# Five accumulating DMAs begun in the last part of the output projection instead of seven in the attention stage

## The chip, the cores and the metric

The kernel runs on one core of one Trainium2 chip. The metric is the device time of one execution in microseconds, given as a median over runs. Engines are named as in the profile: PE (TensorE matmul), PEld (TensorE weight load), DVE (VectorE), ACT (ScalarE), POOL (GpSimd) and SP (SyncE, which here only starts transfers).

## What is computed

One decoder layer on x of 256 tokens by 2048 channels, float32, batch 1:

```
h    = rmsnorm(x, pre_mix_g);  proj = h @ w_in             # 2048 x 4368
o_a  = sliding-window attention with sinks and ALiBi (16 heads)
o_b  = forgetting attention (16 heads, gate from proj)
mix  = concat(rmsnorm(o_a, grp_swa_g), rmsnorm(o_b, grp_fox_g)) @ w_out   # 2048 x 2048
x    = x + rmsnorm(mix, post_mix_g)
u    = causal_dwconv(rmsnorm(x, pre_ffn_g) @ w_up)          # 2048 x 11264, width 3
gate, val = split(u)
x    = x + rmsnorm((gelu(gate) * val) @ w_down, post_ffn_g)    # 5632 x 2048
```

## The kernel before

**Stages.** Weights stream from HBM in pieces of 512 KB through five buffers called `raw`; ACT rounds each to a high part `whi` and DVE makes the rest `wlo`, and PE multiplies with both. The order of the stages is w_in with both attentions (up to about 276 us), w_out (its first half of rows, for group A, from about 238 us, and its second half from about 276 to 334 us), w_up with convolution and GELU in two halves, each followed by two column passes over w_down.

**The sums of w_down blocks.** The column passes use a scheme with fewer products for 14 pairs of 128-row blocks of w_down, 7 in each half (`FAST`). For each pair it needs four combinations of quarter blocks, which are built in DRAM ahead of time: SP copies two blocks into scratch tensors `t13` and `t24` (line 87), and then POOL starts four accumulating DMAs (line 94) which add DRAM to DRAM: two from w_down into `t13`, one from `t13` into `t24`, and one within `t24`. The trace calls all of these `t`; in the order of the program the first pair has `t_74` (its t13) and `t_75` (its t24), the second pair `t_76` and `t_77`, and so on to `t_101`. The third add of a pair reads what the first wrote, and the fourth reads what the third wrote; POOL waits for these by the semaphores of the earlier adds before it starts the later one.

**What sets the place of an add.** `w_load` counts the weight loads. While the count lies in a span of `ADDS`, each load adds the span's pace to a debt, and when the debt reaches the size of the next add in the list (2 for 512 KB, 1 for 256 KB), that add is put into POOL's program there and kept in program order:

```
    def begin_some(steps, span):
        begin, end, pace = span
        if begin <= loads[0] < end:
            owed[span] = owed.get(span, 0) + pace
            while steps and owed[span] >= steps[0][0]:
                size, step = steps.pop(0)
                owed[span] -= size
                tc.keep_in_program_order(step())
```

The list is one for the whole kernel, so what one span doesn't take, the next one begins with. Loads 1 to 73 are of w_in, 74 to 89 of the first half of w_out's rows, 90 to 105 of the second half (four for each block of 512 output columns), and from 106 on of w_up.

**The second half of w_out.** `out_half(1, evac_b, range(2))` does column blocks 0 and 1. `evac_b` reads a finished bank: DVE adds it to the first half's result `mix` (line 792), ACT sums its squares (line 793), POOL multiplies it by the gain `gbc` (line 794). Blocks 2 and 3 are done in an order written out by hand for ACT, DVE and POOL: the piece (tokens 0, block 2), the piece (tokens 0, block 3), then `mix_rstd(0)`, whose last step is a power on POOL (line 239, `rmix`), then `residual(0, n)` for four n on DVE (line 812, `x_sb`), then `turn(0, n)`, which transposes `x_sb` on PE (line 819). PE's order is the program's. The same is done for tokens 1, and then w_up begins (lines 998, 1002, 340, 346), whose convolution has a multiply on POOL for each of 88 channel blocks (line 963).

Of the kernel before, what the change touches and what calls it, by code (L numbers as in the profile page):

```python
# [25 lines left out]
FHALF = 22  # L26
HOLD = 3
COPIES = (13, 91, 11 / 8)
ADDS = (30, 75, 1 / 4), (112, 282, 9 / 16)
FAST = (0, 2, 3, 4, 5, 6, 7)  # L30
FULL = (6, 7)

# [2 lines left out]
def hybrid_layer(ctx: ExitStack, tc: tile.TileContext, x, pre_mix_g, w_in, b_forget, sinks,  # L35
# [66 lines left out]
# [9 lines that stand above are left out]
    def w_load(src, a, c, pin=False):  # L111
# [5 lines left out]
        if not paused[0]:  # L117
            begin_some(copies, COPIES)
            for span in ADDS:
                begin_some(adds, span)  # L120
# [1284 lines left out]
```

## Time and profile before

| | |
|---|---|
| median of 3 runs | 1055.83 us (1054.78 to 1055.93) |
| the profiled execution, its own time | 1054.8 us |
| its span | 1053.1 us |
| busy: PE, DVE, ACT, POOL | 1041.0, 844.3, 659.8, 272.5 us |
| accumulating DMAs (line 94) | 56, of them 46 of 512 KB and 10 of 256 KB |

Times in the trace count from the start of the span. A row of the timeline gives start, duration, engine, line, operation, output and input names with shapes, how many, and in brackets the idle time of that engine before it with what ended it. A row of windows gives the stretch, its length, the busy time of each engine with the number of instructions, the granted clock of PE, the mean busy share of the 16 DMA engines and GB/s. "DMA to landing" is the time from the start of the issuing instruction to the arrival of the data.

### The profile page before, as it was taken

The page shows a single profiled execution, that of the slowest core. Times are in us where ns is not written, and L with a number is a line of the kernel's source. Part 1 is how long each engine was busy: PE and PEld are TensorE (multiplying, and loading weights), DVE is VectorE, ACT ScalarE, POOL GpSimd, SP SyncE. Part 2 cuts the span into 40 slices and gives each one's busy share as a digit, 9 for nine tenths or more (in the row PEclk, how much of TensorE's full clock was granted, in tenths as well). Part 3 has the DMA queues.
Part 4 walks back from the last instruction along what each step waited for, and adds up shares of the span by engine and source line. Part 5 has one row for each costly group of instructions (what it writes and reads, how often), then busy time and mean ns, then how long its engine had stood idle before and what let it go on. Part 6 is the DMA issues. An engine that isn't in the chain of part 4 may idle for free.

```text
span 1053.1 us, 16574 instructions
## 1 busy us (share of the span) xinstructions
PE 1041.0 (99%) x5854; PEld 907.6 (86%) x5854; DVE 844.3 (80%) x1370; ACT 659.8 (63%) x1126; POOL 272.5 (26%) x312
## 2 busy tenths in 40 slices
PE   9999999999999999999999999999999999999996
PEld 7889988888889988888888888888888888888885
DVE  5988887787467887788868799867788878779997
ACT  6766666676655865566556675646656666568771
POOL 4254325442022224232223000013223323210004
PEclk9999999999999999999999999999999999999999
DMA  8978999988872899899999796889999999969893
GB/s 281 314 246 289 295 300 308 359 251 303 319 257 68 265 252 260 230 269 240 228 242 265 259 410 196 290 234 222 287 223 247 254 230 257 235 221 387 292 419 130
DMA packets 177470, 279.98 MB, mean 266 GB/s; under 512 B 9052, under 2 KB 133244, under 8 KB 176124
## 3 DMA queue, kind: packets, MB, share of 16 engines
q1 hardware_dynamic: 162432, 249.51, 69.3%
q0 software_dynamic: 13952, 26.74, 17.3%
q10 hardware_dynamic: 1004, 2.68, 0.6%
q8 instruction: 46, 0.75, 0.3%
q14 instruction: 36, 0.29, 0.1%
HBM read 274.55 MB, written 57.69 MB: 315 GB/s over the span
## 4 chain that ended last, share of the span: by engine, by line
PE 89%; DVE 4%; DMA 3%; ACT 1%; POOL 1%; issue 1%; SPq 0%; DVEq 0%; POOLq 0%; ACTq 0%
PE bank_acc L340 16%; PE bank_att L340 14%; PE bank_acc L365 12%; PE bank_att L1044 10%; PE bank_acc L346 8%; PE bank_att L346 7%; PE bank_acc L309 7%; PE bank_acc L1044 5%; PE bank_acc L314 4%; DMA spare<-t 1%; PE bank_att L531 1%; PE bank_att L566 1%; DVE wlo L171 1%; PE bank_acc L1002 1%; DMA spare<-in_w_down_dram 1%; DVE wlo L369 1%
## 5 line engine op out<-in xcount | busy, mean ns | idle before, releaser
L171 DVE TENSOR_TENSOR wlo<-raw,whi 128x1024 fp32r<-128x1024 f32 (+3 forms) x271 | 335.8, 1251 | 94.7 <-ACT whi L168 86.4
L168 ACT CAST whi<-raw 128x1024 fp32r<-128x1024 f32 (+3 forms) x270 | 273.6, 1029 | 102.1 <-issue 43.8
L963 POOL TENSOR_TENSOR room<-room,rowf 128x256 f32<-128x256 f32 x88 | 97.7, 1132 | 331.3 <-DVE room L962 329.5
L340 PE MATMUL bank_acc<-hT,whi 128*128 128x512 f32 x736 | 173.3, 390 | 0.0
L340 PEld LDWEIGHTS bank_acc<-hT,whi 128*128 128x128 f32 x736 | 136.4, 188 | 27.4
L340 PE MATMUL bank_att<-hT,whi 128*128 128x512 f32 x640 | 150.6, 390 | 0.0
L340 PEld LDWEIGHTS bank_att<-hT,whi 128*128 128x128 f32 x640 | 118.7, 188 | 23.9
L967 ACT ACTIVATE room<-room,cw 128x256 f32<-128x256 f32 x88 | 52.7, 601 | 68.9 <-POOL room L963 68.6
L346 PEld LDWEIGHTS bank_acc<-hT,wlo 128*128 128x128 f32 x736 | 89.3, 188 | 2.0
L346 PE MATMUL bank_acc<-hT,wlo 128*128 128x256 f32 x736 | 89.9, 279 | 0.0
L309 PE MATMUL bank_acc<-hT,whi 128*128 128x512 f32 x352 | 88.0, 395 | 0.0
L1044 PE MATMUL bank_att<-whi,G 128*128 128x512 f32 x258 | 87.8, 389 | 0.0
L365 PE MATMUL bank_acc<-whi,oT 128*128 128x512 f32 (+1 forms) x272 | 81.7, 379 | 0.0
L346 PEld LDWEIGHTS bank_att<-hT,wlo 128*128 128x128 f32 x640 | 77.6, 188 | 1.7
L369 DVE TENSOR_TENSOR wlo<-raw,whi 128x1024 fp32r<-128x1024 f32 (+1 forms) x66 | 71.6, 1105 | 9.3 <-ACT whi L368 8.4
L346 PE MATMUL bank_att<-hT,wlo 128*128 128x256 f32 x640 | 77.9, 279 | 0.0
L973 DVE SCALAR_TENSOR_TENSOR room<-room,cw 128x256 f32<-128x256 f32 x88 | 60.2, 686 | 21.7 <-ACT room L967 21.7
L368 ACT CAST whi<-raw 128x1024 fp32r<-128x1024 f32 (+1 forms) x66 | 61.8, 953 | 22.5 <-DMA raw<-in_w_down_dram 5.7
L309 PEld LDWEIGHTS bank_acc<-hT,whi 128*128 128x128 f32 x352 | 63.3, 188 | 11.6
L365 PEld LDWEIGHTS bank_acc<-whi,oT 128*128 128x128 f32 x272 | 50.2, 188 | 9.3
L1044 PEld LDWEIGHTS bank_att<-whi,G 128*128 128x128 f32 x258 | 48.4, 188 | 10.0
L365 PE MATMUL bank_acc<-wlo,oT 128*128 128x512 f32 (+1 forms) x136 | 51.2, 377 | 0.0
(269 smaller groups left out, 1760.9 us busy)
## 6 DMA issues: line engine op xcount, KB each, us to landing
raw<-in_w_up_dram SPq DMA_DIRECT2D x176, 512.0 KB, 5.6
raw<-in_w_in_dram SPq DMA_DIRECT2D x51, 512.0 KB, 7.2
raw<-in_w_down_dram SPq DMA_DIRECT2D x45, 512.0 KB, 7.2
raw<-in_w_out_dram SPq DMA_DIRECT2D x32, 512.0 KB, 6.1
t<-in_w_down_dram POOLq DMA_DIRECT2D x28, 512.0 KB, 8.7
raw<-t SPq DMA_DIRECT2D x26, 512.0 KB, 6.6
t<-t POOLq DMA_DIRECT2D x18, 512.0 KB, 8.7
extra<-t SPq DMA_DIRECT2D x14, 512.0 KB, 6.3
```

The costliest lines, as they stand in the source:

```text
L168: i1 = act.copy(hi[:, cs], raw[:, cs])
L171: i2 = dve.tensor_tensor(lo[:, cs], raw[:, cs], hi[:, cs].bitcast(F32), op=ALU.subtract)
L309: pe.matmul(b, parts[u][0][:, a, m * P:(m + 1) * P], hT[:, kt, :], start=(kt == 0), stop=(kt == KT - 1))
L340: pe.matmul(b, parts[u][0][:, a, m * P:(m + 1) * P], hT[:, kt, :], start=(kt == 0), stop=(kt == KT - 1))
L346: pe.matmul(b[:, 256:512], parts[u][1][:, a, m * P:(m + 1) * P], hT[:, kt, 0:256], start=False, stop=False)
L365: pe.matmul(b, a, r[:, cols], start=(first and i == 0), stop=(last and i == 2))
L368: act.copy(hi, src)
L369: dve.tensor_tensor(lo, src, hi.bitcast(F32), op=ALU.subtract)
L963: pool.tensor_tensor(u[:, 2:258], u[:, 2:258], rowf, op=ALU.mult)
L967: act.activation(y, u[:, 2:258], AF.Identity, bias=cw[:, 3, ch:ch + 1], scale=cw[:, 2, ch:ch + 1])
L973: dve.scalar_tensor_tensor(y, u[:, 1:257], cw[:, 1, ch:ch + 1], y, op0=ALU.mult, op1=ALU.add)
L1044: pe.matmul(b[:, to] if to else b, a, r[:, cols], start=(first and i == 0), stop=(last and i == 2))
```

## The change

One line of numbers. The first span of `ADDS` goes from loads 30 to 74 at a quarter for each load to loads 92 to 102 at three quarters:

```
-ADDS = (30, 75, 1 / 4), (112, 282, 9 / 16)
+ADDS = (92, 103, 3 / 4), (112, 282, 9 / 16)
```

Before, the first span has 45 loads, a debt of 11.25, and begins seven adds (sizes 2, 2, 1, 2, 1, 2, 1). Now it has 11 loads, a debt of 8.25, and begins the first five of them, at loads 94, 97, 98, 101 and 102; the sixth and seventh and all later ones move back by two places in the list of the second span. The order of the instructions on PE, DVE and SP stays the same; on ACT one weight cast changes places with a cast of attention keys.

POOL in the attention stage: `p` are the attention tables, `sqs` sums of squares, `scr` scaled projections; a row with - is of before, one with + of now.

```order
 L622 TENSOR_SCALAR p<-scr 128x256
 L623 TENSOR_SCALAR p<-scr 128x128
-L609 TENSOR_TENSOR sqs<-sqs,sqo 128x256
-L94 DMA t_74<-in_w_down_dram 256x512
-L609 TENSOR_TENSOR sqs<-sqs,sqo 128x256 x2
-L94 DMA t_74<-in_w_down_dram 256x512
-L498 TENSOR_TENSOR scr<-scr 128x256 x2
+L609 TENSOR_TENSOR sqs<-sqs,sqo 128x256 x3
+L498 TENSOR_TENSOR scr<-scr 128x256 x2
+L609 TENSOR_TENSOR sqs<-sqs,sqo 128x256
```

The adds have left POOL's queue there, and the other five of this stage are gone in the same way.

POOL in the second half of w_out, before: `mix_sb` rows are the multiplies by the gain, in the order block 0 (two), block 1 (two), tokens 0 of block 2 and of block 3, then the power `rmix`. In brackets stands what a row waits for: Activation, DVE, PE and Pool are semaphores of the engines, DMAHWn of SP's transfers, and DMASWn that of the add number n, counted from 0, and again from 0 after 7.

```order
L794 TENSOR_TENSOR mix_sb<-mix_sb,gbc_mix 128x512 [waits DMAHW1_49,Activation_49]
L794 TENSOR_TENSOR mix_sb<-mix_sb,gbc_mix 128x512 [waits Activation_49] x5
L239 TENSOR_TENSOR rmix_3821<-rv,mhalf 128x1 [waits DVE_49]
L794 TENSOR_TENSOR mix_sb<-mix_sb,gbc_mix 128x512 [waits Activation_49]
L794 TENSOR_TENSOR mix_sb<-mix_sb,gbc_mix 128x256 [waits Activation_49] x2
```

The same place now:

```order
L794 TENSOR_TENSOR mix_sb<-mix_sb,gbc_mix 128x512 [waits DMAHW1_49,Activation_49]
L794 TENSOR_TENSOR mix_sb<-mix_sb,gbc_mix 128x512 [waits Activation_49]
L94 DMA t_74<-in_w_down_dram 256x512 x2
L794 TENSOR_TENSOR mix_sb<-mix_sb,gbc_mix 128x512 [waits Activation_49] x2
L94 DMA t_75<-t_74 128x512 [waits DMASW0_49]
L94 DMA t_76<-in_w_down_dram 256x512
L94 DMA t_75<-t_75 128x512 [waits DMASW2_49]
L794 TENSOR_TENSOR mix_sb<-mix_sb,gbc_mix 128x512 [waits Activation_49] x2
L239 TENSOR_TENSOR rmix_3819<-rv,mhalf 128x1 [waits DVE_49]
```

Two adds now stand between the multiplies of block 0 and of block 1, and three between those of block 1 and of block 2; the last of the three waits for the first of the three, with only one issue between them, and the multiplies of blocks 2 and 3 and `rmix` stand behind it.

POOL at the end of the second half of w_up, before (`room` rows are the multiplies of the convolution):

```order
L94 DMA t_100<-in_w_down_dram 256x512 [waits DMASW5_49]
L963 TENSOR_TENSOR room<-room,rowf 128x256 [waits DVE_49] x2
L94 DMA t_101<-t_100 256x512 [waits DMAHW2_49,DMASW3_49]
L94 DMA t_101<-t_101 256x512 [waits DMASW6_49]
L963 TENSOR_TENSOR room<-room,rowf 128x256 [waits DVE_49] x6
```

The same place now:

```order
L94 DMA t_100<-in_w_down_dram 256x512 [waits DMASW5_49]
L963 TENSOR_TENSOR room<-room,rowf 128x256 [waits DVE_49] x2
L94 DMA t_101<-t_100 256x512 [waits DMAHW2_49,DMASW3_49]
L963 TENSOR_TENSOR room<-room,rowf 128x256 [waits DVE_49] x2
L94 DMA t_101<-t_101 256x512 [waits DMASW6_49]
L963 TENSOR_TENSOR room<-room,rowf 128x256 [waits DVE_49] x2
```

The last add stands two pairs of multiplies later, with a pair between it and the one that it waits for.

## Prediction

> **What bounds the kernel now.** I read the page first, then the windows, to see where PE isn't busy, then PE's waits.
>
> ```profile
> span 1053.1 us, 16574 instructions
> PE 1041.0 (99%) x5854; PEld 907.6 (86%) x5854; DVE 844.3 (80%) x1370; ACT 659.8 (63%) x1126; POOL 272.5 (26%) x312
> ```
> ```profile
> 0.00:10.00 10.00, 7.76 (x24) 5.01 (x25) 4.11 (x9) 5.20 (x10) 9.06 (x23) 1.00 0.80 254
> 10.00:130.00 120.00, 119.86 (x793) 110.53 (x793) 99.33 (x234) 84.99 (x198) 42.39 (x45) 1.00 0.87 287
> 130.00:140.00 10.00, 9.46 (x57) 7.98 (x56) 9.64 (x20) 9.36 (x19) 0.00 (x0) 1.00 0.94 322
> 140.00:180.00 40.00, 40.00 (x252) 34.68 (x251) 29.20 (x60) 24.75 (x49) 17.06 (x24) 1.00 0.99 306
> 180.00:190.00 10.00, 9.95 (x62) 8.57 (x62) 6.76 (x14) 5.88 (x14) 8.55 (x15) 1.00 1.00 295
> 190.00:1040.00 850.00, 850.00 (x4644) 737.10 (x4643) 687.12 (x1024) 527.90 (x835) 191.03 (x204) 1.00 0.88 262
> 1040.00:1053.00 13.00, 3.95 (x33) 3.75 (x32) 8.18 (x14) 1.74 (x6) 4.43 (x5) 0.80 0.44 161
> ```
> ```profile
> PE bank_att L578 <- DVE pl L369: 0.5, 1, 0.5
> ```
>
> PE is the bound at a full granted clock. Of its 12.1 us without work, 2.2 are the start and 9 the end, which the change doesn't touch. From 10 to 190 us it idles for 0.14 + 0.54 + 0.05 = 0.73 us, and from 190 to 1040 us for none at all. Two things follow. The most that the change can win is 0.73 us, 0.07% of the time, since that is all that the stage it relieves has to give; the largest of those waits was ended by DVE, not by a transfer. And any stall that the change makes on PE after 190 us is added to the end in full, since nothing behind it has idle time to take it up. A measurement of this kernel can tell about 0.2%, 2.1 us, from no change.
>
> **What leaves the attention stage.** Seven issues on POOL, the first and the last of them here:
>
> ```profile
> 118.80 1.11 POOL L94 DMA_DIRECT2D t<-in_w_down_dram  x1
> 229.34 0.83 POOL L94 DMA_DIRECT2D t<-t  x1
> ```
>
> About 0.9 us of POOL each, and 2.75 MB of transfers spread over 110 us. POOL is a quarter busy and PE waits for nothing here but the 0.73 us; so I count the gain at 0, with 0.73 us as its end. The swapped casts on ACT are about 1 us apart in time with PE unstalled around them: 0 too.
>
> **What comes into w_out.** The order decides here, and these are POOL's rows there, then the DVE and PE rows that depend on them.
>
> ```profile
> 303.95 1.91 POOL L794 TENSOR_TENSOR mix_sb<-mix_sb,gbc_mix 128x512 f32<-128x512 f32 x1 [0.32 <-ACT junk L793]
> 311.30 2.53 POOL L794 TENSOR_TENSOR mix_sb<-mix_sb,gbc_mix 128x512 f32<-128x512 f32 x2 [5.43 <-ACT junk L793]
> 317.24 1.29 POOL L794 TENSOR_TENSOR mix_sb<-mix_sb,gbc_mix 128x512 f32<-128x512 f32 x1 [3.41 <-ACT junk L793]
> 322.68 1.29 POOL L794 TENSOR_TENSOR mix_sb<-mix_sb,gbc_mix 128x512 f32<-128x512 f32 x1 [4.15 <-ACT junk L793]
> 323.93 0.55 POOL L239 TENSOR_TENSOR rmix<-rv,mhalf 128x1 f32<-128x1 f32 x1
> ```
> ```profile
> 324.51 2.74 DVE L812 SCALAR_TENSOR_TENSOR x_sb<-mix_sb,rmix,x_sb 128x512 f32<-128x512 f32 x4 [1.54 <-POOL rmix L239]
> 326.05 1.03 PEld L819 LDWEIGHTS bank_att<-ident,x_sb 128*128 128x128 f32 x8
> 326.28 1.04 PE L819 MATMUL bank_att<-ident,x_sb 128*128 128x128 f32 x8
> ```
>
> The chain multiply, power, residual, transpose ends on PE with little to spare. The first residual is done at 324.51 + 0.69 = 325.20 (2.74 / 4 each) and its transposes load from 326.05 on: 0.85 us of slack. The second is done 0.69 later and wanted 0.52 later (half of the 1.03), so the slack that counts is 0.85 - 0.17, about 0.7 us.
>
> The first two adds are issued behind the second multiply of block 0, at 303.95 + 1.91 = 305.86, and are through POOL well before 311.30: nothing late. The third add stands behind the multiplies of block 1, which end at 313.83, and waits for the first; the fifth waits for the third. So two landings in a row set when POOL gets on, and these are the rows for a landing:
>
> ```profile
> t<-in_w_down_dram POOLq DMA_DIRECT2D x28, 512.0 KB, 8.7
> t<-t POOLq DMA_DIRECT2D x10, 256.0 KB, 9.9
> ```
> ```profile
> DMA to landing us min/median/max: 5.3/8.8/13.1
> ...
> DMA to landing us min/median/max: 8.8/8.8/8.8
> ```
> ```profile
> 903.76 0.90 POOL L94 DMA_DIRECT2D t<-t  x1
> 912.79 0.87 POOL L94 DMA_DIRECT2D t<-t  x1 [8.14 <-DMA t<-t]
> 913.37 1.66 POOL L963 TENSOR_TENSOR room<-room,rowf 128x256 f32<-128x256 f32 x2
> ```
>
> The landing lines are of all 56 adds and of the one at 903.76 alone. The last three rows show the very thing that the change makes in w_out: an add that waits on POOL for the add just before it, 8.14 us long. That add landed after 8.8 us, and the next one started 9.03 us after it, so a wait costs the landing and 0.2 us more; the multiply behind started 0.58 us after the second add. At that place it cost nothing: POOL's next multiply came in time.
>
> First landing, 512 KB at the median 8.7: the third add starts at 305.86 + 8.7 + 0.2 = 314.8. Second landing, 256 KB: between the 5.3 of the fastest of all 56 and the 13.1 of the slowest. The median of its kind, 9.9, is of stretches in which the DMA engines are full; here they weren't:
>
> ```profile
> 306.00:314.00 8.00, 8.00 (x37) 6.63 (x36) 4.63 (x5) 2.50 (x5) 2.53 (x2) 1.00 0.92 301
> 314.00:320.00 6.00, 6.00 (x28) 4.95 (x27) 2.23 (x2) 1.67 (x3) 1.29 (x1) 1.00 0.01 3
> ```
>
> From 314 to 320 us they stand still now; only the second and fourth add will share them with the third. I take the middle of the fastest and the median, 7.6 us, since the quiet speaks for less and the other two adds (1 MB) for more. Then the fifth add starts at 314.8 + 7.6 + 0.2 = 322.6, the two multiplies behind it run from 323.2 (0.58 later) and take 1.25 each, and `rmix` starts at 325.7 in place of 323.93, 1.75 us late. Less 0.7 of slack, PE stalls for 1.05 us, say 1.1. In one line: the stall is the second landing less 6.55 us. With 5.3 there is none; with the median 9.9 it is 3.3 us; with 13.1 it is 6.5.
>
> Is a second stall behind it? The same chain for tokens 1 begins with work of PE and DVE that is late by the same amount, so it moves along and adds nothing; only DVE is 0.7 us later against PE than before.
>
> ```profile
> 336.64 2.74 DVE L812 SCALAR_TENSOR_TENSOR x_sb<-mix_sb,rmix,x_sb 128x512 f32<-128x512 f32 x4 [0.66 <-POOL rmix L239]
> 338.41 1.80 PE L819 MATMUL bank_att<-ident,x_sb 128*128 128x128 f32 x15
> ```
>
> The fourth residual is done at 339.38, and the last four of 16 transposes begin about 1.4 us after 338.41, at 339.8: 0.4 us of slack, so at most 0.3 us more, if DVE makes up nothing; I take 0. Loads of w_up that share the engines with the adds are early: nothing on PE waits for a weight transfer here.
>
> [...]
>
> **What moves in w_up.** The sixth and seventh add and all later ones come at most two multiply pairs later. The last one now stands behind the pair at 923.53, and the reading of the sums goes on until long after:
>
> ```profile
> 923.53 2.31 POOL L963 TENSOR_TENSOR room<-room,rowf 128x256 f32<-128x256 f32 x2 [8.50 <-DVE room L962]
> 960.82 0.33 SPq L113 DMA_DIRECT2D raw<-t  x1
> ```
>
> Issued at 925.8 and landed by 939 even at 13.1 us, it is read by one of the last two or three of the pass's 14 loads of sums, not before 960.82. So 20 us cover it: 0. Where an add waits for one issued a pair earlier, POOL's 8.50 us of idle time ahead of a pair hides up to that much: 0 as well.
>
> **The sum.** 1054.8 (the profiled execution's own time) - 0 + 1.1 + 0 = 1055.9 us. That execution is 1.0 us below the median of the runs, 1055.83, so I forecast 1055.83 + 1.1 = 1056.9 us for the median: nothing that can be measured, with a small loss in it.
>
> **Rivals.**
>
> Slower, by one mechanism: the second landing isn't helped by the quiet, because the second add's 512 KB are still in the queue ahead of it and the fourth's beside it, and takes its median or more. From 8.65 us on (6.55 + 2.1) the loss can be measured. At 9.9 the time is 1055.83 + 3.3 = 1059.1, at 13.1 it is 1062.3. For it: the median of ten; against it: the empty engines from 314 us on.
>
> No stall: the adds land so fast on empty engines, at or under 6.55 us, that POOL waits behind nothing, and the attention stage gives back up to 0.73 us: 1055.1 to 1055.8. For it: the 5.3 us of the fastest add, and the engines at 0.01. Against it: only the fastest of 56 is known to be so low. [...]
>
> A late sum: the later adds hold up a multiply of the convolution or a load in a column pass. There the price would be one such wait, 8.14 us less what idle time takes, 1057 to 1064. Against it: 8.5 us of idle time ahead of the multiplies and 20 us before the reading.
>
> Faster by over 0.2%: needs 2.1 us, and PE has 0.73 us to give. Only something that this trace doesn't show could do it.
>
> **How the numbers follow.** A stall of up to 2.1 us: 0.44. No stall: 0.20. The long landing: 0.28. A late sum that can be measured: 0.04. Faster: 0.04. So within 0.2%: 0.64; slower: 0.32; faster: 0.04. The range begins at 1055.0, no stall and most of the attention's waits gone, and ends at 1060.2, a second landing of about 11 us (1055.83 + 11.0 - 6.55 = 1060.3); what lies above (the slowest landings, a late sum) and below is 2 in 10.
>
> **What would show it.** In the trace after: an idle time of POOL of about 7 us ahead of the fifth add, put down to an add before it; the two multiplies of `mix_sb` behind it with no gap between them; `rmix` about 1.8 us later against PE's work; and on PE a wait of about 1 us at line 819 for DVE's `x_sb`, the only new one. The 0.54 us at line 578 stays. If POOL's wait ends before 322 us, the no-stall rival holds; if PE's wait at line 819 is over 2 us, the long landing does. A wait of PE anywhere after 360 us would prove me wrong on w_up.

## The result, and the profile after

The changed kernel takes 1060.92 us in the median of seven runs (1058.89 to 1064.51); the kernel before, on the same chip, 1055.63 us in seven (1054.44 to 1056.10). The ratio is 1.0051 with a 95% interval of [1.0039, 1.0064]: slower by half a per cent, 5.3 us. The profiled execution took 1059.44 us. Forecast were 1056.9 us and a range to 1060.2, so the time lies just above the range, on the side of the rival named the long landing.

The head of the page of the changed kernel: the work of PE has not grown by more than half a microsecond, its span by 4.6.

```profile
span 1057.7 us, 16573 instructions
PE 1041.5 (98%) x5854; PEld 907.3 (86%) x5854; DVE 842.6 (80%) x1370; ACT 661.2 (63%) x1126; POOL 277.3 (26%) x312
```

PE's waits in it (line waited for, us in total, times, longest). The new one is the first; the wait at L578 is as it was.

```profile
PE bank_att L819 <- DVE x_sb L812: 4.0, 1, 4.0
PE bank_att L578 <- DVE pl L369: 0.5, 1, 0.5
```

POOL's timeline in w_out of the changed kernel. The two waits on landings stand in brackets (3.22 and 6.87 us), and the two multiplies with `rmix` come straight behind the second.

```profile
305.00 2.07 POOL L94 DMA_DIRECT2D t<-in_w_down_dram  x2
309.97 2.54 POOL L794 TENSOR_TENSOR mix_sb<-mix_sb,gbc_mix 128x512 f32<-128x512 f32 x2 [2.91 <-ACT junk L793]
315.73 0.83 POOL L94 DMA_DIRECT2D t<-t  x1 [3.22 <-DMA t<-in_w_down_dram]
316.28 1.19 POOL L94 DMA_DIRECT2D t<-in_w_down_dram  x1
324.35 0.81 POOL L94 DMA_DIRECT2D t<-t  x1 [6.87 <-DMA t<-t]
324.89 2.76 POOL L794 TENSOR_TENSOR mix_sb<-mix_sb,gbc_mix 128x512 f32<-128x512 f32 x2
327.34 0.84 POOL L239 TENSOR_TENSOR rmix<-rv,mhalf 128x1 f32<-128x1 f32 x1
```

PE's timeline behind it: the first group of transposes, the second and the third.

```profile
329.02 1.77 PE L819 MATMUL bank_att<-ident,x_sb 128*128 128x128 f32 x8 [3.97 <-DVE x_sb L812]
...
334.58 1.03 PE L819 MATMUL bank_att<-ident,x_sb 128*128 128x128 f32 x8
...
342.96 1.91 PE L819 MATMUL bank_att<-ident,x_sb 128*128 128x128 f32 x16
```

Between the first group and the second lie 5.56 us. In the kernel before the same stretch ran from 326.28 to 330.03, 3.75 us. The windows of the changed kernel say why: the granted clock, the number behind the five engines, is at one half just there.

```profile
328.00:330.00 2.00, 0.97 (x6) 0.74 (x7) 1.79 (x3) 0.53 (x1) 0.18 (x1) 0.93 0.83 191
330.00:332.00 2.00, 2.00 (x11) 2.00 (x10) 2.00 (x4) 2.00 (x8) 0.00 (x0) 0.50 0.17 35
332.00:334.00 2.00, 2.00 (x15) 2.00 (x14) 2.00 (x7) 1.20 (x5) 0.72 (x1) 0.72 0.10 14
334.00:336.00 2.00, 2.00 (x20) 2.00 (x19) 2.00 (x6) 0.64 (x3) 0.62 (x2) 1.00 0.78 248
```

So this execution lost 3.97 us of waiting and 5.56 - 3.75 = 1.81 us of slow work, 5.8 in all. PE had come to this place 1.2 us earlier than in the profile of before (325.05 against 326.28); about 1.0 us of that is there by 13 us, before anything that the change touches. 5.8 - 1.2 = 4.6 is what the spans show. Behind 334.58 nothing is lost: the third group comes 4.55 us later than before, as the second does.

The windows that stand in the prediction for 306 to 320 us read like this now, with the DMA share and GB/s at the end (a packet counts in the window in which it starts, so a share can be over 1):

```profile
306.00:314.00 8.00, 8.00 (x37) 6.61 (x36) 3.73 (x5) 2.50 (x5) 3.60 (x4) 1.00 1.01 188
314.00:320.00 6.00, 6.00 (x28) 4.97 (x27) 2.33 (x3) 1.67 (x3) 1.74 (x2) 1.00 1.10 277
320.00:326.00 6.00, 5.05 (x23) 3.85 (x21) 0.71 (x3) 3.77 (x5) 1.65 (x2) 1.00 0.95 122
```

The quiet stretch is gone: a share of 0.01 has become 1.10. From 306 to 314 us the full engines move 188 GB/s where they moved 301. The adds have pushed loads of w_up into the stretch that was empty, and one of them shows it best. Line 113 issues SP's loads; first the fifth load of w_up in the trace of before, then in the trace of after:

```profile
L113 SPq DMA_DIRECT2D raw<-in_w_up_dram x1: 368/368/368, 309.8 to 309.8; - x1
...
DMA to landing us min/median/max: 4.9/4.9/4.9
```
```profile
L113 SPq DMA_DIRECT2D raw<-in_w_up_dram x1: 843/843/843, 308.4 to 308.4; - x1
...
DMA to landing us min/median/max: 20.7/20.7/20.7
```

It lands at 329.1 in place of 314.7, and ACT's cast of it, which stood at 326.48 before, starts at 329.47.

### The profile page after: what moved, and what is told of

Same layout as the page of the kernel before. It is cut to its first block, busy times and chain, and to the rows that moved or that the text cites. A ratio compares the mean times of both kernels' runs of the same rounds, so it can differ in the third digit from the quotient of the medians.

```text
span 1057.7 us, 16573 instructions
## 1 busy us (share of the span) xinstructions
PE 1041.5 (98%) x5854; PEld 907.3 (86%) x5854; DVE 842.6 (80%) x1370; ACT 661.2 (63%) x1126; POOL 277.3 (26%) x312
## 4 chain that ended last, share of the span: by engine, by line
PE 81%; DMA 7%; DVE 6%; ACT 2%; issue 1%; POOL 1%; SPq 0%; DVEq 0%; POOLq 0%; ACTq 0%
PE bank_acc L340 16%; PE bank_att L340 14%; PE bank_acc L365 9%; PE bank_acc L346 8%; PE bank_att L346 7%; PE bank_acc L309 7%; PE bank_att L1044 7%; PE bank_acc L314 4%; PE bank_acc L1044 4%; DMA spare<-t 1%; DMA extra<-t 1%; DVE more L369 1%; PE bank_att L531 1%; DMA t<-in_w_down_dram 1%; DVE wlo L369 1%
## 5 line engine op out<-in xcount | busy, mean ns | idle before, releaser
L346 PEld LDWEIGHTS bank_acc<-hT,wlo 128*128 128x128 f32 x736 | 89.3, 188 | 2.0
L346 PE MATMUL bank_acc<-hT,wlo 128*128 128x256 f32 x736 | 89.8, 279 | 0.0
L346 PEld LDWEIGHTS bank_att<-hT,wlo 128*128 128x128 f32 x640 | 77.6, 188 | 1.7
L346 PE MATMUL bank_att<-hT,wlo 128*128 128x256 f32 x640 | 77.9, 279 | 0.0
```

What stands on the lines that cost most here:

```text
L346: pe.matmul(b[:, 256:512], parts[u][1][:, a, m * P:(m + 1) * P], hT[:, kt, 0:256], start=False, stop=False)
```

## The experiments

Three causes had to be told apart: **A**, POOL's wait for the adds' chain holds `rmix`; **B**, the adds' traffic makes the fifth load of w_up late; **C**, the clock that falls behind a wait. All ratios are to the kernel before in the same comparison, with 95% intervals.

**No adds in w_out, the later ones as after.** The first five adds stay in the attention stage, the sixth and seventh go to w_up as in the changed kernel.

```
-ADDS = (30, 75, 1 / 4), (112, 282, 9 / 16)
+ADDS = (30, 66, 1 / 4), (112, 282, 9 / 16)
```

> The kernel before with a shorter first span, so that five adds begin in the attention stage and none in w_out; w_up gets exactly the adds of the changed kernel. Both theories of w_out (POOL's wait; the late load): 1054.7 on a chip whose kernel before takes 1054.7, nothing lost. Later-adds theory: 1060.

Measured: 1055.45 us, 1.0001 [0.9991, 1.0010], and no new wait on PE. The shift of the later adds costs nothing. The loss is in w_out.

**The wait without the traffic.** The kernel before, with ten multiplies on POOL whose result nobody reads, put between the multiplies of blocks 1 and 2; no adds in w_out.

```
+        for i in range(10):
+            pool.tensor_tensor(sqs.rearrange("p a s -> p (a s)"), mix[1][1], gbc[:, 512:1024],
+                               op=ALU.mult)
```

> The kernel before, with ten multiplies on POOL that nobody reads between the multiplies of blocks 1 and 2, about 12.8 us of work in place of the wait, and no add in w_out. Queue theory: they end at about 326.6 us in the time of the trace of before, rmix starts at 329.1 in place of 323.9, and PE stalls for 5.2 - 0.7 = 4.5 us: 1060. Transfer theory: no transfer is added, 1055.6. Later-adds theory: 1055.6.

Measured: 1064.93 us, 1.0090 [1.0075, 1.0106]. POOL's timeline, PE's wait and the windows behind it in this run:

```profile
312.95 14.43 POOL L855 TENSOR_TENSOR sqs<-mix_sb,gbc_mix 128x512 f32<-128x512 f32 x10
...
329.79 0.55 POOL L239 TENSOR_TENSOR rmix<-rv,mhalf 128x1 f32<-128x1 f32 x1
```
```profile
PE bank_att L819 <- DVE x_sb L812: 5.7, 1, 5.7
```
```profile
330.00:332.00 2.00, 0.82 (x4) 0.83 (x5) 1.63 (x3) 0.00 (x0) 0.33 (x1) 0.50 0.00 0
332.00:334.00 2.00, 2.00 (x11) 2.00 (x10) 2.00 (x4) 1.67 (x7) 0.00 (x0) 0.50 0.00 0
```

A late `rmix` alone makes the same picture with the DMA engines empty (share 0.00): the wait at L819, then half the clock, then a second group 5.75 us behind the first. The dose was larger than meant, 14.43 us for an expected 12.8, and the wait with it. The execution with the trace is the fastest of the six (1062.09 us); what the others lost beyond it is not shown.

**The adds without their chain.** The list of adds is put in another order, so that the four begun in w_out are four of 512 KB that wait for none of each other. The bytes are the same 2.0 MB.

```
-ADDS = (30, 75, 1 / 4), (112, 282, 9 / 16)
+ADDS = (92, 103, 3 / 4), (112, 282, 9 / 16)
+    adds[0:7] = [adds[i] for i in (0, 1, 3, 5, 2, 6, 4)]
```

> The list of adds is put in another order, so that four adds of 512 KB from w_down begin in w_out and none waits for another; the same 2 MB move there, the last at the same load. Queue theory: POOL waits for no DMA in w_out, 1055 to 1056.5. Transfer theory: the whole loss stays, 1060 to 1061, and ACT waits 3 us or more for a raw of w_up before the first transposed pieces. Later-adds theory: 1060.

Measured: 1056.00 us, 1.0011 [1.0002, 1.0019]. POOL waits for no landing; PE waits 0.7 us at the transposes, with the clock at 1.00 throughout, though the fifth load of w_up still takes 18.0 us to land. Most of the loss goes with the chain; a tenth of a per cent stays. The run is not a clean test of A alone: without the chain the third and fourth add are issued from 312.3 us on and not from 315.7, no add starts later, and the load lands at 326.3 us in place of 329.1, just in time for ACT (its cast starts at 326.72).

**One add fewer.** Four adds in w_out; the fifth, which waits for the third, goes to the start of w_up, where no `rmix` is behind it.

```
-ADDS = (92, 103, 3 / 4), (112, 282, 9 / 16)
+ADDS = (92, 102, 3 / 4), (112, 282, 9 / 16)
```

> The first four of the five adds stay in w_out; the fifth, which waits for the third, goes to the start of w_up, behind the second rmix. Queue theory (the loss is POOL's wait for the third add, with the multiplies and rmix behind it): the loss of 5.3 us goes, 1055 to 1056.5, and PE's wait of 4 us at line 819 is gone. Transfer theory (the loss is 2 MB of adds on the DMA engines, which make the loads of w_up late for ACT): 1.75 of the 2 MB are still there, so 4 us or more of loss stay, 1059.5 to 1061, with ACT waiting for raw as now. Later-adds theory (the loss is in w_up): still 1060.

Measured: 1058.49 us, 1.0027 [1.0016, 1.0039]; the queue theory, which gave 1055 to 1056.5, is not enough. `rmix` is on time (323.12) and the first group of transposes waits for nothing. The wait has come up again at the third group; ACT's and PE's timeline of this run, then the windows there:

```profile
330.09 1.05 ACT L168 CAST whi<-raw 128x1024 fp32r<-128x1024 f32 x1 [4.72 <-PE bank_att L819]
331.04 2.16 ACT L824 ACTIVATE hT<-bank_att,gcol 128x128 fp32r<-128x128 f32 x8
333.04 0.68 ACT L793 ACTIVATE junk<-mix_sb 128x512 bf16<-128x512 f32 x1
```
```profile
340.70 3.48 PE L819 MATMUL bank_att<-ident,x_sb 128*128 128x128 f32 x16 [2.53 <-DVE x_sb L812]
```
```profile
340.00:342.00 2.00, 1.30 (x7) 1.06 (x8) 2.00 (x4) 0.56 (x3) 0.00 (x0) 0.79 0.28 84
342.00:344.00 2.00, 2.00 (x12) 2.00 (x11) 2.00 (x7) 2.00 (x9) 0.00 (x0) 0.50 0.04 10
```

This is B. The fifth load of w_up is issued at 309.3 and lands 20.4 us later, at 329.7; the row names PE as what ended ACT's idle time, but the load is what came last. Its cast stands ahead of the transposed pieces (L824) and of the sums of squares of tokens 1 (L793) in ACT's order, so those run 3.6 us late (331.04 against 327.43, 333.04 against 329.44), and with them the second `rmix` and PE. In the changed kernel A comes first, and B is hidden behind it: nothing is lost there at the third group.

**The cast out of the way, with and without the chain.** Both kernels take the cast of that load behind the last L824 in ACT's order, the one with five adds in w_out, the other with four.

```
+            val.append(w_split(w_load(w_rows(w_up, 0, 4, DFF, 256), 4, 256), still=True))
...
-                    proj_T4(w_up, DFF + c0, bv)
+                    proj_T4(w_up, DFF + c0, bv, val[0])
```

Five adds, cast moved:

> The changed kernel, but ACT's cast of the fifth w_up load, which isn't wanted before the value columns, is put behind the last transposed pieces on ACT, where a late load holds up nothing. POOL's wait for the adds stays. Late-load theory alone: 1055 to 1056. POOL-wait theory alone: 1060, no change. Both, one behind the other: POOL's wait still makes PE wait about 4 us at the first transposes, so 1059 to 1060.5, and hardly anything is gained, since the second wait was hidden behind the first.

Measured: 1060.73 us, 1.0054 [1.0039, 1.0070]. POOL's wait is 7.36 us, PE's at L819 3.4 us, and the clock falls as before (0.50 from 330 to 332 us). Its profile also has two waits at L346 for DVE's `wlo` in w_up (2.0 us in all, the longer at 386 us), which the trace of after has not, so this run doesn't say that A alone costs exactly as much as both.

Four adds, cast moved:

> The cast moved in the same way, in the kernel with four adds in w_out, where POOL's wait at rmix is gone and PE waited 2.5 us at the third group of transposes. Late-load theory: the 3.8 us go, 1054.7 to 1055.7, no wait of PE at line 819 or its like. If something else of the 1.75 MB costs: 1057.5 to 1058.5 as with the four adds alone.

Measured: 1056.04 us, 1.0008 [1.0000, 1.0016]. No wait at L819, the clock at 1.00, though the load took 20.0 us to land. So the four cases, all with the adds' bytes in w_out, are: neither 1.0008, B alone 1.0027, A alone 1.0054, both 1.0051. A and B don't add up; whichever comes first covers the other.

**Does the load's delay go with the bytes?** Two adds (1 MB) in w_out; the second span's pace is raised so that all adds are begun in the end.

```
-ADDS = (30, 75, 1 / 4), (112, 282, 9 / 16)
+ADDS = (92, 98, 3 / 4), (112, 282, 0.6)
```

> The kernel before with its first span of adds set to loads 92 to 98 at three quarters, so that only two adds (1 MB) are begun in w_out, and the second span's pace raised to 0.6 so that all are begun in the end. No add of w_out waits for another. Shared-engine theory (the fifth load of w_up lands late because the adds' bytes take the engines that it needs, so the delay goes with the bytes): it lands about 10 to 13 us after its issue in place of 18 to 21 with four or five adds and 4.9 with none, which is before ACT wants it at about 326 us; no wait on PE at L819; time 1055 to 1056, a ratio of 0.999 to 1.001. Rival (the load's delay doesn't go with the bytes, any add ahead of it is enough): landing 18 us or more, ACT's cast at about 329 to 330 us, a wait on PE of 2 to 3 us at the third group of L819, time 1057.5 to 1058.5.

Measured: 1054.97 us, 0.9997 [0.9987, 1.0007]. The fifth load of w_up, and ACT's cast of it, in this run:

```profile
L113 SPq DMA_DIRECT2D raw<-in_w_up_dram x1: 368/368/368, 309.1 to 309.1; - x1
...
DMA to landing us min/median/max: 12.1/12.1/12.1
```
```profile
325.83 1.05 ACT L168 CAST whi<-raw 128x1024 fp32r<-128x1024 f32 x1 [0.31 <-PE bank_acc L365]
```

It lands at 321.2, before ACT wants it, and nothing is late. With 0, 1.0, 1.75 and 2.0 MB of adds the load took 4.9, 12.1, 20.0 to 20.4 and 18.0 to 20.7 us: an estimated 6.5 to 9 us of delay for each MB, though from 1.75 to 2.0 MB it no longer grows. The 12.1 us lie where the shared-engine theory had them (10 to 13); by what means the adds slow the load no run here shows.

**The clock.** The changed kernel with 14 unread products of 128x512 on PE just ahead of the first transposes, in the time in which it would wait.

```
+            for i in range(14 if t == 0 and n == 0 else 0):
+                pe.matmul(tb, oT[8][:, 0:P], kept[3][0][1], start=True, stop=True)
```

> The changed kernel with 14 matmuls of 128x512 that nobody reads in PE's queue just ahead of the first transposes, 3.2 us of work in a wait of 4. If the time were the wait alone: 1060.9, no change, or a little more where the wait is short. If the granted clock, which falls to 0.50 for some 4 us after the wait, adds to it (about 1.7 us by the 28.02 against 32 us of windows): the clock stays at 1.00 and the time falls by 1 to 2 us, to 1059 to 1060.

Measured: 1059.34 us, 1.0039 [1.0026, 1.0053]. PE's timeline, then a window, of this run:

```profile
324.30 3.33 PE L818 MATMUL bank_att<-whi,oT 128*128 128x512 f32 x14
328.29 1.32 PE L821 MATMUL bank_att<-ident,x_sb 128*128 128x128 f32 x8 [0.65 <-DVE x_sb L812]
...
332.32 1.04 PE L821 MATMUL bank_att<-ident,x_sb 128*128 128x128 f32 x8
```
```profile
330.00:332.00 2.00, 2.00 (x19) 2.00 (x18) 2.00 (x4) 2.00 (x8) 0.00 (x0) 1.00 0.04 10
```

`rmix` is as late as in the changed kernel, but PE stays busy, the clock stays at 1.00, and the second group comes 4.03 us behind the first in place of 5.56. The traces price the clock's fall at 1.5 us. The medians agree (1.0051 to 1.0039 is 1.3 us; 5.3 us over before against 4.2), though their intervals overlap.

**How long a wait brings it down.** The kernel before with eight unread multiplies on POOL, and with seven (the edit of the ten, with another number).

> The run with ten unread multiplies on POOL in w_out, with eight instead; no adds in w_out. Ten took 14.43 us and made PE wait 5.71 us at L819. Eight take 11.5 us, so rmix starts at about 326.9 and PE waits 2.8 us. Clock theory (an idle of PE of 2.5 us or more is followed by some 4 us at a granted clock of 0.5, which costs 1.3 to 2 us more): clock at 0.5 behind the wait, second group of L819 5.3 to 5.8 us behind the first, time 4 to 4.8 us over before. Rival (the wait alone is the loss, and the slow clock in the rows is hidden in it): 2.5 to 3 us over before.

Measured with eight: 1059.51 us, 1.0045 [1.0031, 1.0059], 4.4 us over before. PE waits 3.0 us, and the clock is at 0.61 and 0.53 from 330 to 334 us. A wait of 3 us alone would have been 1.0028, below the interval.

> The same with seven unread multiplies: they take 10.1 us, rmix starts at about 325.5 and PE waits 1.4 us at L819, between the 0.72 us that left the clock alone and the 2.53 us that brought it down. If the clock needs an idle of more than about 2 us to fall: clock 1.00 throughout, second group 3.75 to 4.1 us behind the first, time 1.2 to 1.7 us over before, a ratio of about 1.0014. If 1.4 us is enough: clock at 0.5 behind it, 2.6 to 3.4 us over before, a ratio of about 1.0028.

Measured with seven: 1058.28 us, 1.0028 [1.0018, 1.0038]. In the profiled execution PE waits 1.7 us and the clock stays:

```profile
PE bank_att L819 <- DVE x_sb L812: 1.7, 1, 1.7
```
```profile
328.00:330.00 2.00, 1.99 (x18) 1.84 (x17) 2.00 (x4) 1.81 (x8) 0.00 (x0) 1.00 0.00 0
```

That execution took 1056.87 us, 1.7 over the median of before; the other seven runs took 1057.46 to 1059.00. The trace says no fall after 1.7 us, the median says 3.1 us lost. Whether the clock fell in the runs without a trace stays open. By the length of a single wait the traces show none after 0.7 and 1.7 us, and a fall after 2.5, 3.0, 3.4, 4.0 and 5.7.

The traces show one thing more than the length of a wait: how much PE stood idle just ahead of a fall. In the changed kernel the clock is at one half for 3.41 us, from 329.72 to 333.13 us; in the run with ten multiplies, by its windows, for 6.8 us in all (0.66, 0.50, 0.50 and 0.63 in windows of 2 us from 328 to 336 us). These are rows for the 3.41 us at one half and for as long a stretch just ahead of them, of the changed kernel, then with eight multiplies:

```profile
326.31:329.72 3.41, 0.69 (x5) 0.46 (x5) 1.51 (x3) 0.25 (x1) 1.87 (x3) 1.00 0.86 190
329.72:333.13 3.41, 3.41 (x16) 3.41 (x17) 3.41 (x6) 3.41 (x11) 0.00 (x0) 0.50 0.15 30
```
```profile
327.03:330.45 3.42, 1.40 (x11) 1.16 (x12) 2.21 (x4) 0.77 (x4) 1.18 (x2) 1.00 0.00 0
330.45:333.86 3.41, 3.41 (x19) 3.41 (x18) 3.41 (x8) 2.07 (x8) 1.26 (x1) 0.50 0.00 1
```

In the changed kernel PE is idle for 2.72 us of the stretch ahead (3.41 less 0.69 of work), with eight multiplies for 2.02 us (3.42 less 1.40). With seven the one wait there is of 1.7 us, and the clock stays. What an idle time between these does, and whether it matters when a wait begins, is not shown.

**The adds earlier.** All five ten loads earlier, at loads 84 to 92, so that `rmix` is far off. The edit is against the changed kernel.

```
-ADDS = (92, 103, 3 / 4), (112, 282, 9 / 16)
+ADDS = (82, 93, 3 / 4), (112, 282, 9 / 16)
```

> The same five adds in the same order with the same two waits, but ten loads earlier: POOL waits where it has 24 us of idle time ahead of the first multiply of w_out. Queue theory: nothing of weight stands behind the wait, 1055 to 1056.5. Transfer theory: 2 MB still collide, now with loads of w_out, which come closer to their use than those of w_up do: 1057 or more. Later-adds theory: 1060, since w_up has exactly the adds of the changed kernel.

Measured: 1061.20 us, 1.0064 [1.0051, 1.0078], no better. POOL's waits (7.22 and 7.39 us between 276 and 294 us) hold up nothing there, but w_out's own weights come late; PE's waits in this run:

```profile
PE bank_acc L365 <- ACT whi L168: 2.3, 2, 1.3
PE bank_acc L365 <- DVE wlo L171: 1.7, 2, 0.9
```
```profile
304.87:308.28 3.41, 1.16 (x5) 0.41 (x3) 2.45 (x3) 3.41 (x4) 0.00 (x0) 1.00 0.31 84
308.28:311.69 3.41, 3.41 (x8) 2.76 (x9) 3.41 (x4) 1.89 (x3) 0.00 (x0) 0.50 0.82 224
```

The queue theory missed again. These waits, in pieces of at most 1.3 us, make 4.0 of the 6.5 us. The windows show where most of the rest went: two of the pieces, 1.31 and 0.95 us with a matmul between them, leave 1.16 us of work in 3.41, and the clock is at one half for the next 3.41 us, which takes up to 1.7 us of work (half of 3.41). Neither piece is as long as the 1.7 us with seven multiplies, after which the clock stayed; together they are. The run changes the place and the loads that are hit at once, so it only says that traffic can do the harm by itself.

No version here beats the kernel before by more than can be measured; two adds in w_out are as good (0.9997).

## Why the prediction was wrong

- **PE is the bound; at most 0.73 us to win; stalls add in full.** Right, but for the clock (below). PE has no new wait after 360 us, the wait at L578 stayed, and what was lost by 334.58 is lost at the end.
- **The attention stage gives nothing; the shift in w_up costs nothing.** Right. With the shift and no adds in w_out the ratio is 1.0001; with the attention stage emptied of adds and two of them in w_out it is 0.9997.
- **The place and the form of the stall.** Right: POOL's idle time ahead of the fifth add is 6.87 us (about 7 forecast), the two multiplies follow without a gap, and PE waits at L819 for `x_sb`.
- **Its size.** Wrong: 3.97 us for 1.1. This step of the sum failed: both landings were taken too short, the first most of all, and (below) a stall was priced at its length alone. From the first issue to the third add took 10.7 us where the sum had 8.9 (the first issue itself was 0.86 us earlier than in the sum), and from the third to the fifth 8.6 for 7.8. That is 2.6 of the missing 2.9 us; PE, which came 1.2 us earlier and so was 0.4 us further ahead of POOL, makes up the rest. The formula "second landing less 6.55" took the first landing as known, and that one was further off than the second.
- **Why the landings were long.** The first, the larger miss, took 10.4 us where the sum had the median of 8.7; it lies in a stretch that was full before as well (0.92), and why it took longer than the median no run isolates. The second took 8.3 for 7.6. For it the sum counted on engines that "stand still" from 314 to 320 us, read from a trace without the adds; with them the share was 1.10. The prediction counted the other adds into the stretch, but not the loads of w_up that the adds push there. That these made the second landing longer is read from the windows and not tested alone. The rival of the long landing had the right direction and the right suspicion of the traffic, but its condition was not met: it needed a second landing of 8.65 us or more. That its sign appeared (a wait of over 2 us at L819), and that its price of 3.3 us lies near the 3.97, is luck.
- **"Loads of w_up that share the engines with the adds are early: nothing on PE waits for a weight transfer here."** Wrong, and the most instructive step. PE wasn't waiting for that load. ACT would, once it landed 14.4 us later than before, and PE's next transposes stood behind ACT. In the changed kernel this costs nothing, because POOL's wait covers it; alone it is 1.0027 against 1.0008.
- **A stall of so many us costs so many us.** Wrong where the granted clock falls, as it did in the traces with waits of 2.53 us and more and after the two pieces of 1.31 and 0.95 us, and not after 1.7 us: in the changed kernel the slow clock costs 1.5 to 1.8 us more (5.56 us between the first two groups of transposes, against 4.03 with PE kept busy and 3.75 before), a term that the sum put at nothing. No wait of PE in the middle of the trace of before is over 0.54 us, so it could not show this there. With it the 3.97 us become 5.8, or 4.6 in the spans, on either side of the 5.3 of the medians.

Open: the changed kernel's seven runs spread over 5.6 us and the seven of before over 1.7, which landings that differ from run to run and now reach PE would explain. It isn't shown: larger sets of before, of 18 to 23 runs, spread over 2.8 to 4.8 us themselves, and only one run of the changed kernel has a trace.

## What to carry to other kernels

Here an add that waited for another one, for 6.87 us, held two multiplies and `rmix` behind it on POOL: look at what stands behind such a wait on its engine, and add up every landing in the chain (10.4 and 8.3 us here), not only the last. The idle stretch of the DMA engines was not idle any more with transfers put ahead of it (a share of 1.10 in place of 0.01): work out which loads are pushed into it, and follow each through the engine that reads it. With four adds ACT's cast of a load that nobody needed yet came 3.6 us late (330.09 against 326.48), and PE stood idle for 2.53 us in the end. Where PE is the bound, don't price a wait at its length alone: in the changed kernel one of 3.97 us cost its length and, by the traces, 1.5 to 1.8 us for the slow clock behind it.

## What was not expected of the hardware

The accumulating DMAs from DRAM to DRAM were dear for SP's loads: with 2.0 MB of them a load of 512 KB took 18.0 to 20.7 us in place of 4.9, and in the changed kernel the engines moved 188 GB/s from 306 to 314 us in place of 301, at a share of 1.01 in place of 0.92. And PE's granted clock fell to one half for about 3.4 us after waits of 2.53, 3.0, 3.4 and 3.97 us, for 6.8 us in and behind one of 5.71, and for 3.41 us after two short ones of 1.31 and 0.95 us close together, but not after 0.65, 0.7 and 1.7.
